# Rows scaled in place and turned by TensorE transposes, and the first key products set between the fourth and the fifth turned tile

## The chip, the cores and the metric

The kernel runs on one core of a Trainium2 chip. The metric is the device time of one execution in microseconds (us), from its start to its end. A profiled execution also has a span, from the first to the last instruction that the profiler recorded; the device time is a little longer than the span. Five engines work side by side, each through its own instructions in their order: PE (TensorE, matrix products; PEld is its weight loads), DVE (VectorE), ACT (ScalarE), POOL (GpSimd) and SP (SyncE, which issues the transfers). An engine whose next instruction waits runs nothing behind it.

## The reference

One layer of a small transformer: 1024 tokens of width 1024, 256 context tokens, everything in float32. The change touches the beginning, which is this part:

```python
def rmsnorm(x, g):
    y = xf * lax.rsqrt(jnp.mean(xf * xf, axis=-1, keepdims=True) + EPS)
    return y * g
def adaln(cond, w, b):
    return jax.nn.silu(cond) @ w + b
def modulate(h, shift, scale):
    return h * (1.0 + scale) + shift
...
hc = modulate(rmsnorm(ctx, g_pre_mix), csh1, csc1)      # context
pc = hc @ w_in[:, :COL_Q]
hx = modulate(rmsnorm(x, g_pre_mix), sh1, sc1)          # tokens
p = hx @ w_in                                           # keys, values, gates, queries, ...
```

So each row of `x` is multiplied by one over its root mean square, and each column (feature) then gets a scale and a shift that come from the condition vector `c` by a product with `w_ada`. Behind this follow a gated linear attention, a short convolution, an output projection and a convolutional feed-forward part, which the change leaves alone.

## The kernel before, in words

Tokens lie in eight tiles of 128 rows (`xs[0]` to `xs[7]`, 128x1024). The products need the features on the partitions, so each tile is turned: eight blocks of 128x128, one for each group of 128 features (`ft` 0 to 7). The turned and normed rows are collected in `xT[0]` (tiles 0 to 3, the half `hf` 0 of 512 tokens) and `xT[1]` (tiles 4 to 7, `hf` 1).

- `rms_diag(xt, eng)` (L250) sums the squares of a tile's rows on ACT (`act(..., AF.Square)`) or on DVE (L257), makes the reciprocal root on POOL (`rstd`, L200 and L201, two instructions), and multiplies the identity by it on POOL (L260). The result `dg` is a 128x128 diagonal.
- `turn(t)` (L328) multiplies each of the eight blocks by that diagonal on PE (L335), which turns and scales in one product; DVE copies one half of the result from the accumulation banks to `xT` (L341), ACT the other half.
- `ada_dot(j, ...)` (L226) makes one block of 128 shift or scale entries by a multiply-and-sum on DVE (L230), from a 512 KB block of `w_ada` loaded for it. Blocks `ft` and `8 + ft` belong to the features `ft`.
- `ada_affine(ft)` (L246) turns these into the final shift and scale in `am`, by two small ACT instructions.
- `norm_ft(ft, hf)` (L343) applies `am` on ACT to one feature group of 512 tokens (tile `t`), rounds it on ACT to the high part `hxh`, and leaves the low part `hxl` (L351, DVE) to be called later as `lo()`. Products in this kernel are made of three float32r products of high and low parts.
- `k_q(ft, hf)` (L353) makes the nine products of one unit: six from `hxh` and three that need `hxl` (L359 and L362), for the keys and the first queries. There are 16 units; `prep(n)` (L390) prepares a unit two ahead of the one that runs: `norm_ft`, one `ada_dot` for the next features, after the second of each pair `ada_affine`, and `lo()`.
- Behind these units come further query products (from L145 at 66.84 us in the trace), the value products, and among them the context tiles: `ctx_load` (L499) makes the diagonals of two context tiles, `ctx_norm` (L504) turns them by products with them (L514).

In this first part ACT, DVE, POOL and PE run their instructions in the order in which the code writes them (`tc.manual_schedule`); on SP the order of the transfers is the scheduler's. The tiles `x` take eight buffers; `xT[1]` and the later blocks of `w_ada` reuse them as they come free.

Of the kernel before, what the change touches and what calls it, by code (L numbers as in the profile page):

```python
# [8 lines left out]
F32 = mybir.dt.float32  # L9
# [11 lines left out]
CT = 256  # L21
# [98 lines left out]
def build(nc, ap, out, dbg=None):  # L120
# [3 lines left out]
    def nm(s="t"):  # L124
        return f"{s}{next(names)}"

    def act(o, i, fn=AF.Copy, **kw):
        return S.activation(o, i, fn, **kw)  # L128
# [20 lines left out]
    with tile.TileContext(nc) as tc, tc.manual_schedule(engines={mybir.EngineType.PE}):  # L149
# [25 lines left out]
        def bank(n):  # L175
            return pools[n][1].tile([P, 512], F32, tag=n, name=nm("ps"))
# [7 lines left out]
        def col(name, j=0, n=1):  # L184
            o, w = COLS[name]
            return cols[:, o + j : o + j + n]
# [57 lines left out]
        bsg = cp.tile([P, KT], F32, name="bsg")  # L244

        def ada_affine(ft):  # L246
            act(am[:, 0, ft, 0:1], gcol[:, ft : ft + 1], AF.Identity, bias=col("bada", ft))
            act(am[:, 1, ft, 0:1], gcol[:, 8 + ft : 9 + ft], AF.Identity, scale=col("g1", ft), bias=bsg[:, ft : ft + 1])

        def rms_diag(xt, eng=None):  # L250

            ss = cp.tile([P, 1], F32, tag="ss", bufs=4, name=nm("ss"))
            junk = pst.tile([P, D], BF16, tag="junk", bufs=1, name=nm("junk"))
            if eng is None:
                act(junk, xt, AF.Square, accum_out=ss)
            else:
                eng.tensor_tensor_reduce(junk, xt, xt, 1.0, 0.0, ALU.mult, ALU.add, ss)  # L257
            r = rstd(ss, 1, 1.0 / D)
            dg = pst.tile([P, P], F32, tag="dg", bufs=4, name=nm("dg"))
            G.tensor_scalar(dg, ident, r[:, 0:1], None, ALU.mult)  # L260
            return dg

        def x_load(src, t):
            xt = px.tile([P, D], F32, tag="x", name=nm("x"))
            SY.dma_start(xt, src[t * P : (t + 1) * P, :])
            return xt
# [61 lines left out]
        def turn(t):  # L328

            hf, ts_ = t // 4, slice(t % 4 * P, t % 4 * P + P)  # L330
            for g in range(2):
                pt = bank((ps_mm, ps_at)[g])
                for j in range(4):
                    ft = 4 * g + j
                    PE.matmul(pt[:, j * P : (j + 1) * P], xs[t][:, ft * P : (ft + 1) * P], dgs[t], start=True, stop=True)  # L335
                for q in range(2):
                    o, i = xT[hf][2 * g + q][:, :, ts_], pt[:, 256 * q : 256 * q + 256].rearrange("p (f t) -> p f t", f=2)
                    if g:
                        act(o, i)
                    else:  # L340
                        V.tensor_copy(o, i)  # L341
# [23 lines left out]
        with tc.manual_schedule(engines={mybir.EngineType.Activation, mybir.EngineType.DVE, mybir.EngineType.Pool}):  # L365
# [11 lines left out]
                V.tensor_copy(cbs[0][:, n * 512 : n * 512 + 512], pb)  # L377
# [32 lines left out]
            V.tensor_scalar(bsc1, col("bada", 8, 8), 1.0, None, ALU.add)  # L410
            V.tensor_tensor(bsg, bsc1, col("g1", 0, 8), ALU.mult)
# [12 lines left out]
            xT[1] = [px.tile([P, 2, 512], F32, tag="x", name=nm("xT")) for _ in range(4)]  # L424
            turn(4)
            for raw, pg in zip((wk0, wq0_), pgs):
                act(pg[0][:, :2], raw[:, :2])
            turn(5)
            for raw, pg in zip((wk0, wq0_), pgs):
                V.tensor_tensor(pg[1][:, :2], raw[:, :2], pg[0][:, :2].bitcast(F32), ALU.subtract)  # L430
            ada_dot(1, 0, adas[1][0])
            lo = norm_ft(0, 0)
            turn(6)
            lo()
            turn(7)
# [33 lines left out]


        aT = pgt.tile([NG, T + CT], F32R, name="aT")
        V.memset(aT[96:NG, :].bitcast(F32), 1.0)
        wgr = pst.tile([NG, 2 * QK], F32, tag="t", bufs=4, name="wgr")
        SY.dma_start(wgr, ap["wg"])
        wgh, wgl = (pgt.tile([NG, 2 * QK], F32R, name=n) for n in ("wgh", "wgl"))
# [18 lines left out]
            act(e, e, AF.Ln, bias=one)  # L494
            V.scalar_tensor_tensor(g, pg, 0.0, e, ALU.min, ALU.subtract)

        cxs, cdg, hch, hcl = [], [], [], []

        def ctx_load():  # L499
            for j in range(NCT):  # L500
                cxs.append(x_load(ap["ctx"], j))
                cdg.append(rms_diag(cxs[j]))

        def ctx_norm(f2):  # L504

            if f2 % 2 == 0:
                hch.append(px.tile([P, 4, CT], F32R, tag="x", name=nm("hch")))
                hcl.append(px.tile([P, 4, CT], F32R, tag="x", name=nm("hcl")))
            tt = pst.tile([P, 2, CT], F32, tag="t", bufs=4, name=nm("t"))
            pt = bank(ps_at)  # L510
            for f1 in range(2):
                ft = 2 * f2 + f1
                for j in range(NCT):
                    PE.matmul(pt[:, f1 * CT + j * P : f1 * CT + (j + 1) * P],  # L514
                              cxs[j][:, ft * P : (ft + 1) * P], cdg[j], start=True, stop=True)
# [1155 lines left out]
```

## Time and profile before

| what | value |
|---|---|
| runs | 1153.4, 1157.13 and 1157.71 us, median 1157.13 |
| profiled execution, device time | 1157.1 us |
| its span | 1155.3 us |
| TensorE clock granted, mean | 0.993 |
| PE busy | 97% of the span |
| DVE, ACT, POOL busy | 76%, 46%, 43% |
| first product with `dg` | 7.72 us |
| first key product | 26.84 us |
| first product behind the 16 units | 66.84 us |

In lines of the timeline the first number is the start in us from the beginning of the span, the second the time from there to the end of the row's last instruction, then engine, line, operation, what it writes and reads, the shapes, and the number of instructions; in square brackets stands how long the engine was idle before and what ended that. A product of two float32 tiles shows as two matrix instructions, a transpose as one.

### The profile page before, as it was taken

Reading aid. Unit: us, or ns where it says so; the run is one execution under the profiler, and the core shown is the slowest. Engines: PE = TensorE matmul, PEld = TensorE weight load, DVE = VectorE, ACT = ScalarE, POOL = GpSimd, SP = SyncE. Lnnn points to the kernel's source line nnn. Section 1 sums busy time; section 2 is a strip of 40 time slices with the busy share of each in tenths; the row PEclk is TensorE's granted clock in tenths of the full one; section 3 lists DMA queues with packets and bytes.
Section 4 is the critical chain, followed back from the end, with each engine's and each line's share of the span. In section 5 each row is a group of like instructions: output and inputs, shape, how many; then the busy total and the mean of one; then the engine's idle time right before and its main releaser. Section 6 shows DMA issues by size and latency. Waiting matters only on the chain. (4 is left out here: it accounts for less than half of the span.)

```text
span 1155.3 us, 16916 instructions
## 1 busy us (share of the span) xinstructions
PE 1120.4 (97%) x6272; PEld 927.1 (80%) x6272; DVE 872.3 (76%) x1182; ACT 528.9 (46%) x957; POOL 498.9 (43%) x467
## 2 busy tenths in 40 slices
PE   8899988999999999999999999999999999999997
PEld 6689977888887878887878788888887888888885
DVE  5876657899778556576888978787878787777676
ACT  6845156644344456655233242433333345544443
POOL 5211012347466111128777868687767780000002
PEclk9999999999999999999999999999999999999999
DMA  9884853522113283232343323232323169978572
GB/s 345 311 277 137 275 143 119 149 63 60 46 44 102 59 280 113 79 110 73 91 146 110 109 92 119 92 110 92 119 91 110 66 208 338 357 250 273 195 245 100
DMA packets 80132, 176.00 MB, mean 152 GB/s; under 512 B 9807, under 2 KB 21711, under 8 KB 80050
## 3 DMA queue, kind: packets, MB, share of 16 engines
q1 hardware_dynamic: 80050, 174.93, 45.9%
q8 instruction: 49, 0.80, 0.3%
q14 instruction: 33, 0.27, 0.1%
HBM read 142.12 MB, written 32.78 MB: 151 GB/s over the span
## 5 line engine op out<-in xcount | busy, mean ns | idle before, releaser
L1343 DVE SCALAR_TENSOR_TENSOR y<-u,cols,y 128x945 f32<-128x945 f32 (+2 forms) x176 | 214.8, 1222 | 3.7 <-ACT y L128 1.3
L145 PE MATMUL ps<-mx,p 128*128 128x512 f32 x440 | 174.3, 396 | 4.1 <-DVE g L1398 2.2
L146 PE MATMUL ps<-mx,p 128*128 128x512 f32 x440 | 173.1, 394 | 0.0
L147 PE MATMUL ps<-mx,p 128*128 128x512 f32 x440 | 173.1, 393 | 0.0
L135 POOL TENSOR_TENSOR p<-rs,p 128x512 fp32r<-128x512 f32 x88 | 115.3, 1314 | 88.3 <-ACT p L128 84.5
L643 POOL TENSOR_TENSOR wl<-wr,wh 128x256 fp32r<-128x256 f32 x64 | 62.0, 998 | 158.9 <-ACT wh L128 158.7
L147 PE MATMUL ps<-p,p 128*128 128x512 f32 x308 | 120.1, 390 | 0.2
L146 PE MATMUL ps<-p,p 128*128 128x512 f32 x308 | 120.0, 390 | 0.0
L145 PE MATMUL ps<-p,p 128*128 128x512 f32 x308 | 119.9, 389 | 0.0
L145 PE MATMUL ps<-hxh,wh 128*128 128x512 f32 x256 | 104.5, 408 | 1.2 <-DVE sc L701 1.2
L145 PEld LDWEIGHTS ps<-mx,p 128*128 128x128 f32 x440 | 83.1, 189 | 27.0 <-ACT u L128 5.7
L230 DVE CUSTOM_DVE_ANT_0 ada<-ada,cb 128x1024 f32<-128x1024 f32 x64 | 80.3, 1265 | 31.3 <-DMA ada<-in_ada 30.7
L146 PE MATMUL ps<-hxl,wh 128*128 128x512 f32 x256 | 100.6, 393 | 0.0
L147 PE MATMUL ps<-hxh,wl 128*128 128x512 f32 x256 | 100.5, 393 | 0.0
L128 ACT ACTIVATE p<-rs 128x512 fp32r<-128x512 f32 x88 | 54.5, 623 | 100.5 <-POOL rs L1193 100.5
L147 PEld LDWEIGHTS ps<-mx,p 128*128 128x128 f32 x440 | 83.1, 189 | 18.6
L146 PEld LDWEIGHTS ps<-mx,p 128*128 128x128 f32 x440 | 83.0, 189 | 18.1
L135 POOL TENSOR_TENSOR p<-wr,p 128x512 fp32r<-128x512 f32 x58 | 76.1, 1312 | 13.0 <-ACT p L128 13.0
L128 ACT ACTIVATE y<-u,cols 128x1024 f32<-128x1024 f32 x22 | 26.6, 1210 | 107.1 <-DVE u L1405 107.1
L145 PE MATMUL ps<-b,p 128*128 128x512 f32 x176 | 69.5, 395 | 0.0
L146 PE MATMUL ps<-b,p 128*128 128x512 f32 x176 | 69.4, 394 | 0.0
L147 PE MATMUL ps<-b,p 128*128 128x512 f32 x176 | 69.4, 394 | 0.0
(277 smaller groups left out, 2598.9 us busy)
## 6 DMA issues: line engine op xcount, KB each, us to landing
ada<-in_ada SPq DMA_DIRECT2D x64, 512.0 KB, 4.6
wr<-in_wu SPq DMA_DIRECT2D x48, 512.0 KB, 4.0
h<-hd SPq DMA_DIRECT2D x77, 256.0 KB, 4.5
hd<-h SPq DMA_DIRECT2D x73, 256.0 KB, 2.2
wdr<-in_wd SPq DMA_DIRECT2D x55, 256.0 KB, 3.7
wdr<-in_wd SPq DMA_DIRECT2D x22, 512.0 KB, 5.9
x<-in_x SPq DMA_DIRECT2D x16, 512.0 KB, 4.4
wr<-in_wb SPq DMA_DIRECT2D x16, 512.0 KB, 3.7
```

Of the source, the lines that this page charges most:

```text
L128: return S.activation(o, i, fn, **kw)
L135: (eng or V).tensor_tensor(lo, raw, hi.bitcast(F32), ALU.subtract)
L145: PE.matmul(ps, lh, rh, start=first, stop=False, skip_group_check=more)
L146: PE.matmul(ps, lh, rl, start=False, stop=False, skip_group_check=more)
L147: PE.matmul(ps, ll, rh, start=False, stop=last, skip_group_check=more)
L230: V.tensor_tensor_reduce(raw, raw, cbs[which], 1.0, 0.0, ALU.mult, ALU.add, dst)
L643: eng.tensor_tensor(lo[:, k : k + 2], raw[:, k : k + 2], hi[:, k : k + 2].bitcast(F32), ALU.subtract)
L1343: V.scalar_tensor_tensor(y3[:, ro, co], u3[:, ri, ci], col("wcf", 9 * p + 3 * (dr_ + 1) + dc + 1), y3[:, ro, co], ALU.mult, ALU.add)
```

## The change

- `rms_diag` becomes `rms_rows`: no diagonal is made; the tile's rows are multiplied by the reciprocal root in place, on DVE or (argument `seng=S`) on ACT. The turns on PE are transposes against the identity, one instruction each. The two context tiles are treated in the same way.
- Sums of squares of tiles 5 and 7 go to DVE with the scaling on ACT; tiles 0 to 3, 4 and 6 have the sum on ACT and the scaling on DVE.
- The code interleaves the first four tiles one at a time with their turns. `norm_ft(0, 0)` and the first unit `k_q(0, 0)` come ahead of most of tiles 4 to 7: `rms_rows` of 4 and 5 and `turn(4)` stand ahead of `k_q(0, 0)`, the rest behind it. In `turn` both halves of tiles 4 to 7 use the two banks of `ps_at`, as the four of `ps_mm` are the key banks by then.
- The two instructions of `ada_affine` go from ACT to POOL (and `bsg` is not needed any more).
- Transfers: the first two blocks of `w_ada` and the first weights are issued ahead of `x` tiles 4 to 7.
- The memset of two rows of `aT` goes from DVE to POOL.

```diff
-        def ada_affine(ft):
-            act(am[:, 0, ft, 0:1], gcol[:, ft : ft + 1], AF.Identity, bias=col("bada", ft))
-            act(am[:, 1, ft, 0:1], gcol[:, 8 + ft : 9 + ft], AF.Identity, scale=col("g1", ft), bias=bsg[:, ft : ft + 1])
+            G.tensor_scalar(am[:, 0, ft, 0:1], gcol[:, ft : ft + 1], col("bada", ft), None, ALU.add)
+            G.tensor_scalar(am[:, 1, ft, 0:1], gcol[:, 8 + ft : 9 + ft], bsc1[:, ft : ft + 1], col("g1", ft), ALU.add, ALU.mult)
...
-        def rms_diag(xt, eng=None):
+        def rms_rows(xt, eng=None, seng=V):
...
             r = rstd(ss, 1, 1.0 / D)
-            dg = pst.tile([P, P], F32, tag="dg", bufs=4, name=nm("dg"))
-            G.tensor_scalar(dg, ident, r[:, 0:1], None, ALU.mult)
-            return dg
+            if seng is V:
+                V.tensor_scalar(xt, xt, r[:, 0:1], None, ALU.mult)
+            else:
+                act(xt, xt, scale=r[:, 0:1])
...
-                pt = bank((ps_mm, ps_at)[g])
+                pt = bank(ps_at if t > 3 or g else ps_mm)
...
-                    PE.matmul(pt[:, j * P : (j + 1) * P], xs[t][:, ft * P : (ft + 1) * P], dgs[t], start=True, stop=True)
+                    PE.transpose(pt[:, j * P : (j + 1) * P], xs[t][:, ft * P : (ft + 1) * P], ident)
...
-            xs += [x_load(ap["x"], t) for t in range(4, 6)]
             adas = {0: [ada_load(j, pa, "a", 16) for j in (0, 8)]}
-            xs += [x_load(ap["x"], t) for t in range(6, NT)]
             wk0, wq0_ = wk_load(0, 2), wq_load(0, 0, pkq, "qh", 2)
+            xs += [x_load(ap["x"], t) for t in range(4, NT)]
...
-            dgs = [rms_diag(xs[t]) for t in range(4)]
+            rms_rows(xs[0])
             V.tensor_scalar(bsc1, col("bada", 8, 8), 1.0, None, ALU.add)
+            rms_rows(xs[1])
             turn(0)
-            dgs.append(rms_diag(xs[4], V))
+            rms_rows(xs[2])
             turn(1)
-            dgs.append(rms_diag(xs[5]))
+            rms_rows(xs[3])
             turn(2)
             ada_dot(0, 0, adas[0][0])
             turn(3)
             ada_dot(8, 0, adas[0][1])
             ada_affine(0)
-            dgs.append(rms_diag(xs[6], V))
-            dgs.append(rms_diag(xs[7]))
             pgs = wk_pages(0), wq_pages(wq0)
-            turn(4)
...
+            rms_rows(xs[4])
+            rms_rows(xs[5], V, S)
+            turn(4)
             k_q(0, 0)
+            rms_rows(xs[6])
+            turn(5)
+            rms_rows(xs[7], V, S)
+            turn(6)
+            ada_dot(1, 0, adas[1][0])
+            turn(7)
...
-                cdg.append(rms_diag(cxs[j]))
+                rms_rows(cxs[j])
...
-                    PE.matmul(pt[:, f1 * CT + j * P : f1 * CT + (j + 1) * P],
-                              cxs[j][:, ft * P : (ft + 1) * P], cdg[j], start=True, stop=True)
+                    PE.transpose(pt[:, f1 * CT + j * P : f1 * CT + (j + 1) * P], cxs[j][:, ft * P : (ft + 1) * P], ident)
```

First ACT, between the rounding of the first unit (`hxh` of features 0, tokens 0 to 511) and that of the second (`hxh` in the last row). Before; `xT<-ps` are the copies of turned tiles, `t` and `hxh` the two steps of `norm_ft`, and the numbers behind the names are those of single buffers:

```order
L128 ACTIVATE t_325<-xT_152,am 128x512
L128 ACTIVATE hxh_323<-t_325 128x512
L128 ACTIVATE xT_288<-ps_335 128x2x128
L128 ACTIVATE xT_289<-ps_335 128x2x128
L128 ACTIVATE xT_288<-ps_350 128x2x128
L128 ACTIVATE xT_289<-ps_350 128x2x128
L128 ACTIVATE t_380<-xT_286,am 128x512
L128 ACTIVATE hxh_323<-t_380 128x512
```

And ACT in the same place now, from the rounding of the first unit on (`junk,ss` is a sum of squares; the four copies of tiles 6 and 7 and the second unit follow behind the last row):

```order
L128 ACTIVATE hxh_250<-t_252 128x512
L128 ACTIVATE junk_269,ss_268<-x_136 128x1024
L128 ACTIVATE x_138<-x_138,rstd_278 128x1024
L128 ACTIVATE xT_260<-ps_289 128x2x128
L128 ACTIVATE xT_261<-ps_289 128x2x128
L128 ACTIVATE junk_306,ss_305<-x_140 128x1024
L128 ACTIVATE xT_260<-ps_319 128x2x128
L128 ACTIVATE xT_261<-ps_319 128x2x128
L128 ACTIVATE x_142<-x_142,rstd_329 128x1024
```

Two sums of squares (tiles 4 and 6) and two scalings (tiles 5 and 7) have moved behind the rounding of the first unit, with the copies of the turned tiles between them.

Then DVE from the low part of the first unit (`hxl`) on, now; `ISA junk,ss` is the sum of squares of tiles 5 and 7, `COPY xT` the copies of turned tiles, `TENSOR_SCALAR x` the scaling of tiles 4 and 6:

```order
L350 TENSOR_TENSOR hxl_251<-t_252,hxh_250 128x512
L258 TENSOR_SCALAR x_136<-x_136,rstd_271 128x1024
L255 ISA junk_276,ss_275<-x_138 128x1024
L255 ISA ss_275 128x1
L340 COPY xT_258<-ps_282 128x2x128
L340 COPY xT_259<-ps_282 128x2x128
L258 TENSOR_SCALAR x_140<-x_140,rstd_308 128x1024
L340 COPY xT_258<-ps_312 128x2x128
L340 COPY xT_259<-ps_312 128x2x128
L255 ISA junk_327,ss_326<-x_142 128x1024
L255 ISA ss_326 128x1
```

Before, DVE had behind the low part of the first unit only the copies of the last tile and the next `ada_dot`:

```order
L351 TENSOR_TENSOR hxl_324<-t_325,hxh_323 128x512
L341 COPY xT_286<-ps_343 128x2x128
L341 COPY xT_287<-ps_343 128x2x128
L230 ISA ada_147,gcol<-ada_147,cb_107 128x1024
L230 ISA gcol 128x1
```

The sums and scalings of tiles 4 to 7 thus alternate between ACT and DVE, each in the engine's one queue. The third place is PE at the first unit: `turn(4)` (a row for each half of a tile) stands ahead of it, and `turn(5)` begins right behind its nine products, ahead of the second unit:

```order
L334 MATMUL ps_282<-ident,x_136 128x128 x4
L334 MATMUL ps_289<-ident,x_136 128x128 x4
L358 MATMUL ps_262<-hxh_250,wah_244 128x512
L358 MATMUL ps_264<-hxh_250,wah_244 128x512
L358 MATMUL ps_266<-hxh_250,wqh_246 128x512
L361 MATMUL ps_262<-hxh_250,wal_245 128x512
L361 MATMUL ps_264<-hxh_250,wal_245 128x512
L361 MATMUL ps_266<-hxh_250,wql_247 128x512
L361 MATMUL ps_262<-hxl_251,wah_244 128x512
L361 MATMUL ps_264<-hxl_251,wah_244 128x512
L361 MATMUL ps_266<-hxl_251,wqh_246 128x512
L334 MATMUL ps_312<-ident,x_138 128x128 x4
```

Tiles 6 and 7 follow behind the last row, and then the second unit. Before, all eight turns stood ahead of the first unit.

More of the change, by code (lines that the diff above doesn't have):

```diff
@@ L242, in ada_affine_ctx @@
             V.tensor_tensor(am[:, 1, ft : ft + 4, 1], am[:, 1, ft : ft + 4, 1], col("g1", ft, 4), ALU.mult)
-        bsg = cp.tile([P, KT], F32, name="bsg")
         def ada_affine(ft):
-            act(am[:, 0, ft, 0:1], gcol[:, ft : ft + 1], AF.Identity, bias=col("bada", ft))
-            act(am[:, 1, ft, 0:1], gcol[:, 8 + ft : 9 + ft], AF.Identity, scale=col("g1", ft), bias=bsg[:, ft : ft + 1])
-        def rms_diag(xt, eng=None):
+            G.tensor_scalar(am[:, 0, ft, 0:1], gcol[:, ft : ft + 1], col("bada", ft), None, ALU.add)
+            G.tensor_scalar(am[:, 1, ft, 0:1], gcol[:, 8 + ft : 9 + ft], bsc1[:, ft : ft + 1], col("g1", ft), ALU.add, ALU.mult)
+        def rms_rows(xt, eng=None, seng=V):
             ss = cp.tile([P, 1], F32, tag="ss", bufs=4, name=nm("ss"))
@@ L420, in build @@
             ada_affine(0)
-            dgs.append(rms_diag(xs[6], V))
-            dgs.append(rms_diag(xs[7]))
             pgs = wk_pages(0), wq_pages(wq0)
-            xT[1] = [px.tile([P, 2, 512], F32, tag="x", name=nm("xT")) for _ in range(4)]
-            turn(4)
             for raw, pg in zip((wk0, wq0_), pgs):
                 act(pg[0][:, :2], raw[:, :2])
-            turn(5)
+            lo = norm_ft(0, 0)
             for raw, pg in zip((wk0, wq0_), pgs):
                 V.tensor_tensor(pg[1][:, :2], raw[:, :2], pg[0][:, :2].bitcast(F32), ALU.subtract)
-            ada_dot(1, 0, adas[1][0])
-            lo = norm_ft(0, 0)
-            turn(6)
             lo()
-            turn(7)
+            xT[1] = [px.tile([P, 2, 512], F32, tag="x", name=nm("xT")) for _ in range(4)]
             pk = [bank(ps_mm) for _ in range(4)]
             pq = [bank(ps_ms) for _ in range(2)]
+            rms_rows(xs[4])
+            rms_rows(xs[5], V, S)
+            turn(4)
             k_q(0, 0)
+            rms_rows(xs[6])
[4 more added lines that the diff above has]
+            turn(7)
             load_ada(2)
@@ L471, in build @@
         aT = pgt.tile([NG, T + CT], F32R, name="aT")
-        V.memset(aT[96:NG, :].bitcast(F32), 1.0)
+        G.memset(aT[96:NG, :].bitcast(F32), 1.0)
         wgr = pst.tile([NG, 2 * QK], F32, tag="t", bufs=4, name="wgr")
@@ L495, in logdecay @@
             V.scalar_tensor_tensor(g, pg, 0.0, e, ALU.min, ALU.subtract)
-        cxs, cdg, hch, hcl = [], [], [], []
+        cxs, hch, hcl = [], [], []
         def ctx_load():
```

1 line of the change is left out of this document (removed).

## The prediction

> **What bounds the kernel now.** I read the page first, then the busy time of the engines by stretches, then who waited for whom on PE, then the timeline of the beginning.
>
> ```profile
> PE 1120.4 (97%) x6272; PEld 927.1 (80%) x6272; DVE 872.3 (76%) x1182; ACT 528.9 (46%) x957; POOL 498.9 (43%) x467
> ```
>
> ```profile
> 26.80:66.80 40.00, 36.10 (x147) 26.31 (x146) 30.73 (x47) 31.82 (x58) 10.18 (x9) 1.00 0.90 311
> 66.80:84.00 17.20, 17.20 (x99) 15.29 (x99) 13.50 (x27) 7.50 (x19) 0.00 (x0) 1.00 0.81 277
> 84.00:125.00 41.00, 41.00 (x336) 40.86 (x335) 27.24 (x61) 18.10 (x53) 5.61 (x8) 1.00 0.51 172
> ```
>
> The columns behind the stretch and its length are the busy time of PE, PEld, DVE, ACT and POOL, then the clock, the DMA share and GB/s. From 66.8 us PE never stops for 58 us, so a microsecond by which the first product at 66.84 moves is a microsecond of the end, and one of PE's work less between 84 and 125 us is too. Ahead of that PE is not the bound. These are its products around the units (`k_q`):
>
> ```profile
> 25.04 2.05 PE L335 MATMUL ps<-dg,x 128*128 128x128 f32 x16 [0.74 <-POOL dg L260]
> 26.84 0.70 PE L359 MATMUL ps<-hxh,wah 128*128 128x512 f32 x2
> ...
> 29.20 0.73 PE L359 MATMUL ps<-hxh,wah 128*128 128x512 f32 x2
> ...
> 64.80 0.62 PE L359 MATMUL ps<-hxh,wah 128*128 128x512 f32 x2
> ...
> 66.84 0.39 PE L145 MATMUL ps<-hxh,wqh 128*128 128x512 f32 x1
> ```
>
> A unit takes PE 2.04 us (64.80 to 66.84), the 15 units behind the first would take 30.6, and they take 66.84 - 29.20 = 37.6. For 7.0 us they wait:
>
> ```profile
> PE ps L359 <- ACT hxh L128: 2.7, 6, 0.9
> PE ps L362 <- DVE hxl L351: 1.0, 2, 0.5
> ```
>
> The recorded waits are only part of it, as PE's ends are modelled, but they name what is late: the rounding on ACT and the low part on DVE. So the beginning is decided by how soon ACT and DVE have the rows of the second half of the tokens, and PE's turns matter only where they stand in that chain.
>
> **The first four tiles.** The prices, from ACT, DVE and POOL in the timeline and from the groups by line:
>
> ```profile
> 4.88 1.06 ACT L128 ACTIVATE junk<-x 128x1024 bf16<-128x1024 f32 x1 [1.68 <-DMA x<-in_x]
> 5.84 0.18 ACT L128 ACTIVATION_READ_ACCUMULATOR junk<-x 128x1 f32 x1
> ...
> 14.28 0.66 ACT L128 ACTIVATE xT<-ps 128x256 f32<-128x256 f32 x2 [2.07 <-PE ps L335]
> ...
> 23.09 0.81 ACT L128 ACTIVATE t<-xT,am 128x512 f32<-128x512 f32 x1
> 23.94 0.63 ACT L128 ACTIVATE hxh<-t 128x512 fp32r<-128x512 f32 x1
> ...
> 28.52 0.63 ACT L128 ACTIVATE hxh<-t 128x512 fp32r<-128x512 f32 x1
> ```
>
> ```profile
> 9.97 0.17 DVE L410 TENSOR_SCALAR bsc<-cols 128x8 f32<-128x8 f32 x1 [2.21 <-DMA cols<-in_cols]
> ...
> 11.31 1.23 DVE L257 CUSTOM_DVE_ANT_0 junk<-x 128x1024 bf16<-128x1024 f32 x1 [0.30 <-POOL dg L260]
> ...
> 16.98 0.75 DVE L341 COPY xT<-ps 128x256 f32<-128x256 f32 x2
> 17.65 1.22 DVE L230 CUSTOM_DVE_ANT_0 ada<-ada,cb 128x1024 f32<-128x1024 f32 x1
> ```
>
> ```profile
> 6.12 0.19 POOL L200 TENSOR_SCALAR rstd<-ss 128x1 f32<-128x1 f32 x1 [5.70 <-DVE cb L377]
> 6.40 0.55 POOL L201 TENSOR_TENSOR rstd<-rstd,small 128x1 f32<-128x1 f32 x1
> 7.04 0.63 POOL L260 TENSOR_SCALAR dg<-ident,rstd 128x128 f32<-128x128 f32 x1
> ```
>
> ```profile
> L128 ACT ACTIVATE y<-u,cols 128x1024 f32<-128x1024 f32 x22 | 26.6, 1210 | 107.1 <-DVE u L1405 107.1
> L1105 DVE TENSOR_SCALAR xn<-x,rstd 128x1024 f32<-128x1024 f32 x7 | 5.3, 754 | 9.7 <-POOL rstd L201 8.1 <-ACT xn L128 1.5
> ```
>
> A sum of squares is 1.15 us on ACT (4.88 to 6.02) and 1.22 on DVE; the root costs 0.95 from the sum's end at 6.02 to the start of what uses it (7.04, less the step between); two copies 0.66 on ACT and 0.75 on DVE; a dot 1.22. The scaling on DVE is the same operation and shape as L1105, 0.75. On ACT no row has it: 1.06 (one pass over the same tile, with a sum) to 1.21 (one with scale and bias); I take 1.06. The diagonal's 0.63 goes, but the 0.75 that replaces it moves to DVE or ACT.
>
> PE's turns, as products and as transposes, each with the product that follows:
>
> ```profile
> 89.98 1.05 PE L514 MATMUL ps<-dg,x 128*128 128x128 f32 x8
> 90.80 0.37 PE L145 MATMUL ps<-wah,hxh 128*128 128x272 f32 x1
> ```
>
> ```profile
> 430.39 1.03 PE L1124 MATMUL ps<-ident,xn 128*128 128x128 f32 x8
> 431.18 0.48 PE L145 MATMUL ps<-woh,mh 128*128 128x512 f32 x1
> ```
>
> Four products with the diagonal hold PE 0.82 us in eight passes, eight transposes 0.79: a transpose is one pass of 0.10 us. But PE has two paces. Passes of L335 by stretch:
>
> ```profile
> 7.70:10.27 2.57, 2.55 (x12) 2.55 (x13) 1.00 1.02 400
> ...
> 13.40:15.45 2.05, 2.05 (x21) 2.05 (x20) 1.00 1.03 412
> ```
>
> After idling, 0.21 us a pass (2.57 us for 12); after some 5 us of steady work little over half of it, though the clock column says 1.00. The new turns come in short pieces, so I price them at 0.21 on the way to the first unit: 1.7 us for a tile, 2.0 with the last one's landing. The Trainium skill (TensorE: Matmul & The Clock Gate, Part 4: PE-mode transpose) says that transposes do not count as work for that gate. No row here shows transposes alone; by its rule the turns stay at the slow pace, as in my sum; were they fast, 1.5 us would come off in the two turns on the path.
>
> Now `bsc1` stands ahead of the scaling of tile 1 on DVE, so that waits for `cols` until 10.1. ACT sums tile 3 behind the copies of `turn(1)`: scaling 0.75, turn 2.0, copies 0.66, sum 1.15, root 0.95, together 5.5, and tile 3's scaling starts at 15.6 and ends at 16.35. DVE then copies tile 2 (0.7), does a dot (1.15), copies tile 3 (0.7) and does the second dot (1.22): 20.1. POOL makes `am`: 0.3, and up to 0.6 behind a subtraction on DVE, say 20.9; ACT's two steps (0.85 and 0.63) end at 22.4. Before, that was 24.57. So the first unit's input is 2.2 us earlier.
>
> **The second half.** From there every step waits for the one before, as each engine's queue alternates. Sum of tile 4 on ACT 1.15, root 0.95, scaling on DVE 0.75, sum of tile 5 on DVE behind it 1.22, root 0.95, scaling on ACT 1.06, copies of `turn(4)` behind it 0.66, sum of tile 6 1.15, root 0.95, scaling on DVE 0.75, copies of `turn(5)` behind it 0.75, sum of tile 7 1.22, root 0.95, scaling on ACT 1.06: 13.6. Then the copies of `turn(6)` free the second bank (0.66), four transposes fill it (0.85), copies 0.66, and the two steps of `norm_ft(0, 1)` 1.45: 17.2 in all. The second unit starts at 22.4 + 17.2 = 39.6 instead of 29.20: **+10.4**. `k_q(0, 0)` and the turns on PE fit into this with room, so the earlier first unit gains nothing. All that is queued behind on DVE, the dots of the next features first, waits too.
>
> **The other 15 units.** `ada_affine` leaves ACT, which takes off at most the 2.7 us for which PE waited for the rounding. Two scalings of context tiles come onto DVE, 1.5. And PE meets the second unit after a gap of three to four us. Such a gap, and the clock behind it:
>
> ```profile
> 156.84 0.79 PE L486 MATMUL ps<-wgh,aT 98*128 98x512 f32 x1 [2.35 <-DVE gc L495]
> ```
>
> ```profile
> 156.80:158.50 1.70, 1.67 (x4) 1.38 (x5) 1.70 (x3) 0.84 (x2) 0.00 (x0) 0.50 0.00 0
> ```
>
> A half clock for some 3.3 us costs 1.6. These three cancel nearly; I keep 37.6 for the 15 units, **0**. The lower bound is PE's own pace, 30.6 and 1.6, that is -5.4; the upper bound comes with the third rival.
>
> **The context tiles.** Sixteen products become transposes: 4 x (0.82 - 0.39) = **-1.7**, in full, since PE is busy for 41.00 of 41.00 us there. The memset of `aT` leaves an idle DVE for an idle POOL: nothing. The transfers are issued in another order, but tile 4 still comes before 16 us (1.4 MB more ahead of a tile that DVE reads at 11.31 before, at the 400 GB/s of the row above, are 3.5 us), and its sum starts at 22: hidden.
>
> The sum: 1157.1 + 10.4 + 0 - 1.7 = **1165.8 us**. The profiled execution (1157.1) stands at the runs' median (1157.13), so nothing is to be corrected. 0.5% is 5.8 us, about what a measurement of this kernel can tell from no change.
>
> **The rivals.**
> 1. Faster: the steps of tiles 4 to 7 overlap, and only ACT's own work lies between the two units. That is 2 x 1.15 + 2 x 1.06 + 4 x 0.66 + 1.45 = 8.5, the second unit at 30.9, and with the 15 units at PE's pace of 30.6 the first product behind them at 61.5: 1157.1 - 5.3 - 1.7 = 1150.1. It decides if the chain is shorter than 6.8 us (29.20 - 22.4). For it speak the 97% of PE on the page, and half the passes for its turns. Against it: each root needs its sum, each scaling its root, and the queues have them in turn. Chance 0.04.
> 2. No change that can be told: the chain is as computed, but the units behind it run without waits, as ACT and POOL have been relieved and transfers have had 10 us to come: -5.4, 1160.4. For it: DVE is busy for 30.73 of 40 us, so it isn't full. Against it: the waits in the units come from DVE's dots, low parts and splits, which stay. Chance 0.20.
> 3. Slower still: `am` on POOL waits for DVE. Rows:
>
> ```profile
> 11.37 1.22 POOL L200 TENSOR_SCALAR rstd<-ss 128x1 f32<-128x1 f32 x1
> ...
> 17.86 2.55 POOL L260 TENSOR_SCALAR dg<-ident,rstd 128x128 f32<-128x128 f32 x1
> ```
>
> The first is a 0.19 us operation that ends just after the DVE sum of 11.31, the second a 0.63 us one beside two of DVE's. If each second `am` waits through a low part and a dot in place of a low part alone, each pair of units is 1.22 later: seven times, +8.5, 1174.3. The Trainium skill (SBUF — State Buffer, Who interferes with whom) calls the port that DVE and GpSimd share an exclusive lock, and names DVE operations with two inputs in SBUF; the first row agrees. Whether POOL gets in between two DVE operations decides. Chance 0.14.
>
> That the change does not do what it says I exclude: the transposes of L1124 are eight records for a tile's eight blocks.
>
> **How the numbers follow.** The forecast has 0.62. Slower by over 0.5% (above 1162.9) are the forecast and the third rival, 0.76; within 0.5% the second, 0.20; faster the first, 0.04. The range leaves out the first rival and the outer half of the third: 1159.5, a little below the second, to 1172.5, where `am` costs most of the third's price.
>
> **What would show it.** Right: the second unit near 39.6 us, ACT waiting for POOL between tiles 4 and 7 and PE idle for some 8 us around 30 to 39; the first product behind the units near 77; the context's transposes at half the products' time. The first four tiles are wrong if the first `hxh` is not within a microsecond of 22.4; the chain is wrong if tiles 5 and 7 are scaled while 4 and 6 are summed; the forecast falls if the second unit starts ahead of 33 us, or the units behind it take under 33 us.

## The result, and the profile after

The changed kernel takes 1172.22 us (median of five runs, 1170.77 to 1174.14) against 1157.13 (five runs, 1153.4 to 1158.16): the ratio is 1.0129, with a 95% interval of 1.0114 to 1.0144. The profiled execution has 1170.77 us and a span of 1168.9, 13.6 more than before. In the timeline of PE these rows answer to those around the units; the first two are the turns of tiles 2 and 3:

```profile
13.91 1.09 PE L334 MATMUL ps<-ident,x 128*128 128x128 f32 x8 [1.40 <-DVE x L258]
16.00 1.97 PE L334 MATMUL ps<-ident,x 128*128 128x128 f32 x8 [1.00 <-DVE x L258]
25.05 1.94 PE L334 MATMUL ps<-ident,x 128*128 128x128 f32 x8 [7.08 <-DVE x L258]
26.64 1.20 PE L358 MATMUL ps<-hxh,wah 128*128 128x512 f32 x2
...
29.93 1.04 PE L334 MATMUL ps<-ident,x 128*128 128x128 f32 x8
32.24 1.06 PE L334 MATMUL ps<-ident,x 128*128 128x128 f32 x8 [1.28 <-DVE xT L340]
35.38 1.66 PE L334 MATMUL ps<-ident,x 128*128 128x128 f32 x8 [2.08 <-ACT x L128]
39.15 1.22 PE L358 MATMUL ps<-hxh,wah 128*128 128x512 f32 x2 [2.11 <-ACT hxh L128]
...
82.09 0.39 PE L145 MATMUL ps<-hxh,wqh 128*128 128x512 f32 x1
```

The first unit begins where it did (26.64 against 26.84), although its `hxh` is ready at 22.14, as `turn(4)` stands ahead of it on PE. Then three turns come one at a time, the second waiting for a bank and the third for a scaling, and the second unit begins at 39.15, not at 29.20: 9.95 us. Behind these waits stand the four scalings of tiles 4 to 7, on DVE and ACT in turn, each of which waited for its root from POOL:

```profile
24.15 0.75 DVE L258 TENSOR_SCALAR x<-x,rstd 128x1024 f32<-128x1024 f32 x1 [1.28 <-POOL rstd L201]
...
30.68 0.75 DVE L258 TENSOR_SCALAR x<-x,rstd 128x1024 f32<-128x1024 f32 x1 [3.75 <-POOL rstd L201]
```

```profile
27.00 1.15 ACT L128 ACTIVATE x<-x,rstd 128x1024 f32<-128x1024 f32 x1 [3.82 <-POOL rstd L201]
...
34.18 1.15 ACT L128 ACTIVATE x<-x,rstd 128x1024 f32<-128x1024 f32 x1 [2.52 <-POOL rstd L201]
```

The first product behind the units comes at 82.09, not at 66.84. Of these 15.25 us the second unit brings 9.95, so the other 15 units bring 5.3: they take 42.94 us, not 37.64. The row of the engines' stretches for exactly these units:

```profile
39.15:82.09 42.94, 36.38 (x136) 27.21 (x136) 31.04 (x48) 26.86 (x42) 21.06 (x19) 0.92 0.72 237
```

POOL, the last busy time ahead of the clock (0.92), has 21.06 us in 19 instructions where the row of 26.80 to 66.80 before had 10.18 in 9. Who waits for it is in the list of waits, for ACT and for PE (who waited, for whom, then us in total, how often, and the longest), and in the timelines of POOL, DVE and ACT:

```profile
ACT t L128 <- POOL am L246: 15.4, 7, 3.6
```

```profile
PE ps L334 <- DVE x L258: 11.4, 5, 7.1
PE ps L358 <- ACT hxh L128: 7.3, 5, 2.1
```

```profile
38.08 0.34 POOL L246 TENSOR_SCALAR am<-gcol,bsc,cols 128x1 f32<-128x1 f32 x1 [2.64 <-DVE gcol L230]
...
42.64 1.78 POOL L245 TENSOR_SCALAR am<-gcol,cols 128x1 f32<-128x1 f32 x1
44.47 1.77 POOL L246 TENSOR_SCALAR am<-gcol,bsc,cols 128x1 f32<-128x1 f32 x1
46.21 0.28 POOL L245 TENSOR_SCALAR am<-gcol,cols 128x1 f32<-128x1 f32 x1
49.72 1.77 POOL L246 TENSOR_SCALAR am<-gcol,bsc,cols 128x1 f32<-128x1 f32 x1 [3.23 <-DVE gcol L230]
```

```profile
43.14 1.21 DVE L230 CUSTOM_DVE_ANT_0 ada<-ada,cb 128x1024 f32<-128x1024 f32 x1
...
44.28 0.68 DVE L350 TENSOR_TENSOR hxl<-t,hxh 128x512 fp32r<-128x512 f32 x1
44.89 1.21 DVE L230 CUSTOM_DVE_ANT_0 ada<-ada,cb 128x1024 f32<-128x1024 f32 x1
46.03 0.08 DVE L230 DVE_READ_ACCUMULATOR2_ANT gcol<- 128x1 f32 x1
```

```profile
46.27 0.82 ACT L128 ACTIVATE t<-xT,am 128x512 f32<-128x512 f32 x1 [3.61 <-POOL am L246]
```

At 38.08, with DVE waiting, the second `am` takes 0.34 us. At 44.47 the same instruction takes 1.77 and ends at 46.24, just behind the dot of 44.89, whose sum is read out at 46.03: by its length it waited through the low part and through the dot behind it. Only then does `t` on ACT start, and with it the next `hxh` that PE waits for. ACT stood 15.4 us for `am`; before, with `am` on ACT itself, it stood 4.9 there for the dot. PE stood 7.3 for `hxh` (2.7 before), 2.1 of them ahead of the second unit.

The context part went as written down. Four transposes and what follows, in the timeline:

```profile
105.29 0.60 PE L514 MATMUL ps<-ident,x 128*128 128x128 f32 x4
105.64 0.37 PE L145 MATMUL ps<-wah,hxh 128*128 128x272 f32 x1
```

They hold PE for 0.35 us where the products held it for 0.82. From the first product behind the units to the first one with a context page (`hch`) it is 37.5 us, not 39.2. What lies behind the units is not equally long in every profiled execution (1086.8 us of the span in the changed kernel, 1082.8 in the one with a cleared column below, which is the same there), so the parts of the beginning are compared by their rows, and whole kernels by the ratios of their runs.

### The profile page after: what moved, and what is told of

Same layout as the page of the kernel before. It is cut to its first block, busy times and chain, and to the rows that moved or that the text cites. A ratio compares the mean times of both kernels' runs of the same rounds, so it can differ in the third digit from the quotient of the medians.

```text
span 1168.9 us, 16743 instructions
## 1 busy us (share of the span) xinstructions
PE 1117.2 (96%) x6192; PEld 921.0 (79%) x6192; DVE 874.5 (75%) x1188; ACT 526.1 (45%) x943; POOL 501.1 (43%) x474
```

## The experiments

Four questions were asked in turn: whether `am` alone is the 5.3 us, whether sums and roots are what holds the second unit, what order and way of scaling each cost by themselves, and what is left on the path. In each, "second unit" is its first product in the timeline of PE, and "units" the time from there to the first product behind them. "The changed kernel" has 39.15, 42.94 and a ratio of 1.0129.

**`am` back on ACT, the rest as changed.**

```diff
-            G.tensor_scalar(am[:, 0, ft, 0:1], gcol[:, ft : ft + 1], col("bada", ft), None, ALU.add)
-            G.tensor_scalar(am[:, 1, ft, 0:1], gcol[:, 8 + ft : 9 + ft], bsc1[:, ft : ft + 1], col("g1", ft), ALU.add, ALU.mult)
+            act(am[:, 0, ft, 0:1], gcol[:, ft : ft + 1], AF.Identity, bias=col("bada", ft))
+            act(am[:, 1, ft, 0:1], gcol[:, 8 + ft : 9 + ft], AF.Identity, scale=col("g1", ft), bias=bsg[:, ft : ft + 1])
...
```

> The changed kernel with one part undone: ada_affine is on ACT again (bsg is back), all else as changed. Theory A: the 5.3 us by which the 15 units behind the first grew (37.64 to 42.94 us) are the second am, which on POOL waits 1.8 to 2.8 us beside a low part and a dot of DVE, seven times, so that t on ACT waits 1.5 to 3.6 us each. Then the 15 units take 37 to 39 us, the second unit stays near 39.2 us, and the time is about 1167 us, 5 us under the changed kernel. Theory B: the units grew because the second unit now meets PE after idling (units of 3.8 us instead of 2.0 at half pace) and because the dots of DVE come later; then the 15 units stay at 42 to 43 us and the time at 1171 to 1173 us.

Measured: ratio 1.0069 (1.0057 to 1.0081), median 1163.95 us; second unit 40.29, units 37.53. The timeline of ACT:

```profile
45.51 0.39 ACT L128 ACTIVATE am<-gcol,bsg,cols 128x1 f32<-128x1 f32 x1 [1.05 <-DVE gcol L230]
45.93 0.82 ACT L128 ACTIVATE t<-xT,am 128x512 f32<-128x512 f32 x1
```

The dot ended at 45.48, `am` stands done at 45.9 and `t` follows at once. The units are 5.4 us shorter, and theory A holds: the other things that theory B named are all still there. But the second unit did not stay at 39.2: it comes 1.1 us later, as ACT now waits for the dot with `am` and rounds the first weights only behind it, so that the first `hxh` ends at 23.01, not at 22.14. So the first product behind the units moves by 4.3 us, from 82.09 to 77.82; the time fell by more than that, and the rest lies behind the units.

**`am` on POOL in the kernel before**, the reverse of that diff there, and nothing else.

> The kernel before with one part of the change alone: ada_affine is on POOL; diagonals, products and order as before. Theory A: am on POOL is late by itself, whatever the order ahead of it: second unit still near 29.2 us, the 15 units 42 to 43 us instead of 37.6, time about 1162 us, 5 us over before. Theory B: am on POOL is late only in the new order: 15 units within 1 us of 37.6, time 1156 to 1158 us.

Measured: ratio 1.0045 (1.0033 to 1.0057), median 1161.95; second unit 28.70, units 42.40. In the timelines of POOL and of ACT:

```profile
34.03 1.77 POOL L246 TENSOR_SCALAR am<-gcol,bsc,cols 128x1 f32<-128x1 f32 x1
```

```profile
35.84 0.81 ACT L128 ACTIVATE t<-xT,am 128x512 f32<-128x512 f32 x1 [3.62 <-POOL am L246]
```

It is the same 1.77, and units that are 4.8 us longer than before, without any of the new order. The first product behind the units comes at 71.10, 4.3 later than before, as the second unit is 0.5 earlier. So `am` on POOL costs some 5 us in the units and 4.3 us at their end, shown from both sides.

**One column cleared on DVE between the low part and the next dot**, in the changed kernel.

```diff
                 lo()
+                if hf:
+                    V.memset(gap, 0.0)
...
```

> The changed kernel with one added instruction per pair of units: DVE clears one column (128x1) between the low part that follows the second dot and the next dot, 0.1 us each. In the changed kernel the second am on POOL ends only with the next dot, 1.77 to 2.82 us. Theory A (POOL gets in as soon as DVE runs an instruction with no two inputs in SBUF): am ends behind the low part, 0.8 us or less in 5 of the 7 pairs, t starts a microsecond earlier, the 15 units take 39 us or less, time 1167 to 1169 us. Theory B (POOL gets in only where DVE stands still, whatever it runs): am still 1.7 us or more, 15 units 42 to 43 us, time 1171 to 1174 us.

Measured: ratio 1.0108 (1.0094 to 1.0123), median 1169.37, which can't be told from the changed kernel's; second unit 39.28, units 42.97. In the timelines of DVE and POOL:

```profile
44.59 1.78 POOL L247 TENSOR_SCALAR am<-gcol,bsc,cols 128x1 f32<-128x1 f32 x1
...
45.02 1.22 DVE L231 CUSTOM_DVE_ANT_0 ada<-ada,cb 128x1024 f32<-128x1024 f32 x1
45.04 0.06 DVE L401 MEMSET gap<- 128x1 f32 x1
```

`am` takes as long as ever, as theory B had it. The clearing shows as 0.06 us on top of the dot's start, so it opened no gap. Theory B's reason, that POOL gets in only where DVE stands still, says more than the rows do. In the changed kernel the first instruction of `am` (L245, at 42.64) waits through a low part and a dot too, but ends at 44.42, when DVE has gone on without a stop from the dot (43.14 to 44.35) to the next low part (44.28). What the six long `am` rows there share is that each ends 0.05 to 0.14 us behind the end of a dot, and none behind a low part. What lets them in there was not tested.

**Sums and roots of tiles 4 to 7 moved ahead**, the scalings left in their places.

```diff
             ada_dot(0, 0, adas[0][0])
+            rs = {4: rms_sum(xs[4])}
             turn(3)
             ada_dot(8, 0, adas[0][1])
+            rs[6] = rms_sum(xs[6])
             ada_affine(0)
...
+            for t in (5, 7):
+                rs[t] = rms_sum(xs[t], V)
             lo()
...
```

> The changed kernel with the sums of squares and the roots of tiles 4 to 7 moved ahead: those of tiles 4 and 6 on ACT stand ahead of the first unit's two steps, those of 5 and 7 on DVE behind the low parts of the first weights; the scalings, turns and units stay in their order, and a second buffer for the squares is added. Theory A (the chain sum, root, scaling, turn of the tiles in turn sets the second unit): of the 17.0 us between the first hxh and the second unit the four sums and roots go, 2 x 1.15 + 2 x 1.22 + 4 x 0.95 = 8.5, and some 2 us come back as the first hxh waits for two sums on ACT, and some 2 more as the turns then stand behind each other on PE and its two banks: second unit at 33 to 36 us instead of 39.15, time 4 to 6 us under the changed kernel, about 1167. Theory B (PE's turns in two banks set it): second unit within 1 us of 39.2, time 1171 to 1173.

Measured: ratio 1.0118 (1.0101 to 1.0135), median 1169.88; second unit 39.34, units 42.90. The theory's number failed. The timelines of POOL and of PE say why:

```profile
21.86 2.33 POOL L246 TENSOR_SCALAR am<-gcol,bsc,cols 128x1 f32<-128x1 f32 x1
```

```profile
28.82 1.20 PE L363 MATMUL ps<-hxh,wah 128*128 128x512 f32 x2
...
32.81 1.29 PE L339 MATMUL ps<-ident,x 128*128 128x128 f32 x8
34.60 1.06 PE L339 MATMUL ps<-ident,x 128*128 128x128 f32 x8 [0.50 <-DVE xT L345]
36.17 1.06 PE L339 MATMUL ps<-ident,x 128*128 128x128 f32 x8 [0.50 <-DVE xT L345]
```

The two sums on DVE held up the first `am` on POOL (2.33 us), so the first `hxh` ended at 25.7 instead of 22.14. And the turns of tiles 5 to 7 stand on PE behind the first unit, which takes 4.0 us, and are 1.6 to 1.8 apart. What the sums gave was lost again ahead of them and behind them.

**Both edits together.**

> Both edits together, on the changed kernel: sums and roots of tiles 4 to 7 moved ahead, and ada_affine on ACT. If the late second unit and the late am are two separate costs, they add: second unit at 33 to 36 us, the 15 units 37 to 39 us, time about 1162 us, 9 to 11 us under the changed kernel. If the units only take up slack that the early second unit leaves (one limit behind both, DVE's dots), the first product behind the units moves less than the sum of the two, to 78 us at best, and the time is 1166 or more.

Measured: ratio 1.0042 (1.0029 to 1.0054), median 1160.74; second unit 37.20, units 37.33. The first product behind the units comes at 74.53, 7.6 us earlier than in the changed kernel, so the units do not merely take up slack. It is more than the two edits gave one at a time (4.3 and nothing), since with `am` on ACT the early sums no longer hold up the first `am`. But with the first `hxh` at 23.3 the second unit still comes at 37.2, behind the 33 to 36 expected. By the rows PE is the next limit: it works through `turn(4)`, the first unit and three turns from 26.41 to 35.1 with no stop longer than 0.5 us. These 8 us that the second unit is still late are read from the rows; no run in this order took them out.

**The old order with scaled rows**: sums and roots where they stood before, each tile scaled right ahead of its turn.

```diff
-            dgs = [rms_diag(xs[t]) for t in range(4)]
+            rs = [rms_sum(xs[t]) for t in range(4)]
...
+            scale_rows(xs[0], rs[0])
             turn(0)
-            dgs.append(rms_diag(xs[4], V))
+            rs.append(rms_sum(xs[4], V))
+            scale_rows(xs[1], rs[1])
             turn(1)
...
```

> The order of the kernel before, with the scaled rows and the transposes of the change: sums and roots of all eight tiles where they stood before, each tile scaled right ahead of its turn (tiles 0 to 3, 5 and 7 on DVE, 4 and 6 on ACT), the context tiles as in the change, ada_affine on ACT. Theory A (what costs the second unit is the new place of tiles 4 to 7 in the program; scaling and transposing rows are cheap by themselves): three scalings more on the way of ACT and DVE to the first unit, 2 us, and the context's transposes -1.7; second unit at 30 to 33 us, time 1155 to 1160 us. Theory B (the scaled rows themselves cost, as each turn now waits for a scaling on DVE or ACT and PE meets the units after idling): second unit at 36 us or later, time 1162 us or more.

Measured: ratio 1.0098 (1.0085 to 1.0111), median 1168.03; second unit 43.66, units 36.59. Theory A fell: in the old order the rows cost more than in the new one. The timeline of DVE and of PE around tile 3:

```profile
18.70 0.76 DVE L357 COPY xT<-ps 128x256 f32<-128x256 f32 x2 [1.21 <-PE ps L351]
19.37 1.22 DVE L230 CUSTOM_DVE_ANT_0 ada<-ada,cb 128x1024 f32<-128x1024 f32 x1
...
20.51 0.75 DVE L262 TENSOR_SCALAR x<-x,rstd 128x1024 f32<-128x1024 f32 x1
...
22.47 0.76 DVE L357 COPY xT<-ps 128x256 f32<-128x256 f32 x2 [1.21 <-PE ps L351]
```

```profile
17.55 1.97 PE L351 MATMUL ps<-ident,x 128*128 128x128 f32 x8 [0.66 <-DVE x L262]
...
21.32 1.97 PE L351 MATMUL ps<-ident,x 128*128 128x128 f32 x8 [1.80 <-DVE x L262]
```

DVE scales a tile, stands for 1.21 us until PE has turned it, copies, and only then scales the next; PE stands meanwhile, 13.9 us in all between its eight turns, and each turn takes 1.97 us, 0.21 to 0.25 a transpose. No engine works ahead.

**The new order with diagonals and products**, `am` on ACT, to take the order alone.

```diff
-            rms_rows(xs[4])
-            rms_rows(xs[5], V, S)
+            dgs.append(rms_diag(xs[4]))
+            dgs.append(rms_diag(xs[5], V))
             turn(4)
             k_q(0, 0)
...
```

> The order of the change with the diagonals and products of before: tiles 0 to 7 are turned by products with a diagonal that POOL makes, tiles 4 to 7 behind the first unit, ada_affine on ACT, the context tiles as in the change. Four cases stand then beside each other for the second unit's start, order by way of scaling: 29.20 (old order, diagonals), 43.66 (old order, scaled rows), 40.29 (new order, scaled rows, am on ACT), and this one. Theory A (the new place of tiles 4 to 7 is what costs): 36 to 41 us, as the sums of tiles 6 and 7 still stand behind the copies of the turn before and the first unit stands between the turns. Theory B (scaling in place is what costs, by the queues of DVE and ACT): 29 to 33 us, and a time of 1153 to 1157 us.

Measured: ratio 1.0095 (1.0075 to 1.0116), median 1166.62; second unit 42.08, units 37.38. That is 1.1 us above theory A's 36 to 41 and far from theory B's 29 to 33: the order costs without any scaling in place. The timeline of ACT:

```profile
30.35 0.66 ACT L128 ACTIVATE xT<-ps 128x256 f32<-128x256 f32 x2 [6.11 <-PE ps L351]
30.90 1.06 ACT L128 ACTIVATE junk<-x 128x1024 bf16<-128x1024 f32 x1
```

The sum of tile 6 could have been made during the 6.11 us for which ACT stood, but it is written behind the copies of tile 4. Since the previous experiment showed that rows in the old order cost as much, neither the order nor the rows alone is the cause. What both have is that a step waits in a queue behind a step of the tile ahead.

**The same rows in the old order, each scaled one tile earlier.** If that is the cause, this should do away with it.

```diff
             scale_rows(xs[0], rs[0])
+            scale_rows(xs[1], rs[1])
             turn(0)
             rs.append(rms_sum(xs[4], V))
-            scale_rows(xs[1], rs[1])
+            scale_rows(xs[2], rs[2])
             turn(1)
...
```

> The kernel of the old order with scaled rows, in which the second unit began at 43.66 us, with each tile's scaling moved ahead of the turn before its own. Theory A (there DVE stands for 1.21 us in every turn, since scaling, transposes and copies of one tile wait for each other on its queue): with the scaling one tile ahead the transposes of a tile run beside the copies of the one before, 1.2 us less for each of six or seven turns, second unit at 35 to 37.5 us, time 1160 to 1163 us. Theory B (the sums and roots set it): second unit at 42 us or later, 1167 us.

Measured: ratio 0.9984 (0.9975 to 0.9994), median 1154.31; second unit 31.48, units 37.00. It is better than theory A had it, and under the kernel before. The timeline of PE and of DVE:

```profile
11.29 6.72 PE L351 MATMUL ps<-ident,x 128*128 128x128 f32 x32 [4.13 <-DVE x L262]
18.82 1.09 PE L351 MATMUL ps<-ident,x 128*128 128x128 f32 x8 [0.80 <-ACT x L128]
```

```profile
15.59 0.74 DVE L262 TENSOR_SCALAR x<-x,rstd 128x1024 f32<-128x1024 f32 x1
16.25 0.75 DVE L357 COPY xT<-ps 128x256 f32<-128x256 f32 x2
16.91 1.22 DVE L230 CUSTOM_DVE_ANT_0 ada<-ada,cb 128x1024 f32<-128x1024 f32 x1
```

PE turns four tiles without a stop and stands 4.5 us between its turns, not 13.9; DVE goes from scaling to copies to dot without waiting. The same instructions in another order are 1.1% apart, some 13 us. Against the kernel before nothing is gained in the beginning itself: the first product behind the units comes at 68.48, 1.6 us later than there, and the transposes of the context make up for it.

**Rows scaled on POOL**, in the old order: `G.tensor_scalar(xt, xt, r[:, 0:1], None, ALU.mult)` in place of the diagonal, so that no step is added to DVE or ACT.

> The old order with scaled rows, the scaling on POOL, where the diagonals were made, so that the queues of DVE and ACT are those of before. What a 128x1024 scaling takes on POOL no run here has shown; the nearest row, a low part of 128x512 with two inputs, took 1.28 us alone and 1.9 beside DVE, so an estimate is 1.3 to 4 us each. At 1.3 the second unit would be near 30 and the time 1155 to 1157; at 4 us POOL alone needs 32 us and 6 for the roots, the second unit comes at 44 us or later, time 1168 or more.

Measured: ratio 1.0092 (1.0077 to 1.0107), median 1167.05; second unit 42.03. The timeline of POOL:

```profile
14.70 2.85 POOL L275 TENSOR_SCALAR x<-x,rstd 128x1024 f32<-128x1024 f32 x1
...
18.59 2.85 POOL L275 TENSOR_SCALAR x<-x,rstd 128x1024 f32<-128x1024 f32 x1
```

2.85 us a tile, between the estimate's ends, and 3.9 with the root: eight of them fill POOL until 37 us. The diagonals, an eighth as wide, took 0.61 to 0.63 us there.

**PE kept busy ahead of the second unit** by nine products whose results are not used, in the changed kernel with `am` on ACT.

```diff
             turn(6)
+            busy(5)
             ada_dot(1, 0, adas[1][0])
             turn(7)
+            busy(4)
...
```

> The changed kernel with ada_affine on ACT, and PE kept busy ahead of the second unit: five products of 128x512 more behind the turn of tile 6 and four behind that of tile 7, into a bank that the second unit starts anew, so that the output does not change. There the second unit took 4.0 us where later ones take 2.04. Theory A (that half pace is on the path): the second unit takes 2.1 to 2.5 us, everything behind it comes 1.5 to 2 us earlier, time about 1162. Theory B (ACT and DVE set the third unit whatever PE does): the second unit is shorter but the third starts within 0.7 us of 44.3, no difference in the time (1163.5 to 1164.5).

Measured: ratio 1.0087 (1.0072 to 1.0102), median 1166.54; second unit 39.41. The stretch of 38 to 42 us, without and with these products:

```profile
38.00:42.00 4.00, 1.89 (x5) 1.42 (x5) 2.99 (x5) 3.75 (x9) 0.69 (x1) 0.50 0.40 137
```

```profile
38.00:42.00 4.00, 2.60 (x11) 1.61 (x9) 2.53 (x5) 3.94 (x10) 1.57 (x1) 1.00 0.48 133
```

The granted clock is 1.00 instead of 0.50, and the third unit begins at 42.07 instead of 44.30. So far theory A. But the first product behind the units comes at 77.62, where it was 77.82: later units wait for ACT and DVE and give it all back, and the time is not shorter (the interval overlaps that without the nine products). By theory B's reason, though later than it said, the half clock is no part of the time lost, as far as the kernel with `am` on ACT shows it.

**The context tiles alone**, scaled and transposed in the kernel before.

```diff
-                cdg.append(rms_diag(cxs[j]))
+                scale_rows(cxs[j], rms_sum(cxs[j]))
...
```

> The kernel before with the context part of the change alone: the two context tiles are scaled on DVE and transposed, tiles 0 to 7 and ada_affine as before. By the prediction's term the sixteen transposes take 1.7 us off PE's work between the first product behind the units and the first with a context page (39.16 us before, 37.5 then); the two scalings on DVE may put 0 to 1.5 us onto the units. Theory A: the scalings are hidden, 1154 to 1155 us, 1.7 under before. Theory B: they are not, 1156 us, no difference.

Measured: ratio 0.9989 (0.9978 to 1.0000), median 1154.5. The stretch from the first product behind the units (66.72) to the first with `hch` (104.2) is 37.5 us, not 39.2; the units take 37.94 against 37.64, so the two scalings cost 0.3 at most. The gain is at the edge of what the runs can tell, and its size that of theory A.

**A version to beat both**: the kernel before, context tiles scaled on ACT and transposed, `am` on DVE.

```diff
-            act(am[:, 0, ft, 0:1], gcol[:, ft : ft + 1], AF.Identity, bias=col("bada", ft))
+            V.tensor_scalar(am[:, 0, ft, 0:1], gcol[:, ft : ft + 1], col("bada", ft), None, ALU.add)
...
```

> A version that may beat both: the kernel before, with the context tiles scaled on ACT and transposed, and ada_affine on DVE right behind the second dot instead of ACT. Theory A: transposes -1.7, and t on ACT no longer waits behind am there, another 0 to 1 us: 1153 to 1155 us. Theory B: am's two small instructions on DVE, 0.2 us each, delay the low parts and the next dots by as much as ACT gains: 1155 to 1157 us.

Measured: ratio 0.9979 (0.9970 to 0.9989), median 1154.25; second unit 28.19, units 37.39. This one is faster than the kernel before by 0.1 to 0.3%. Its interval and that of the rows one tile ahead overlap; the two were not joined.

## Why the prediction was right, and where it was not

The direction was right and the time inside the range, but near its upper end: 1172.22 is 6.4 us above the forecast, 0.3 below the end of the range, and nearer to the third rival's 1174.3 than to the forecast. The range was said to leave out the outer half of the third rival, which would have ended it at 1170.1; the end written down, 1172.5, leaves out only the outer 1.8 us. So the forecast was right for a little over half of the loss (8.7 of 15.1 us), and that the range holds the rest is owed to where its end was put. By the prediction's own steps:

- **The first four tiles**: the first `hxh` was to end at 22.4 us and ends at 22.14. Right, also in that the earlier input of the first unit gains nothing.
- **The second half**: the chain was to take 17.2 us and the second unit to start at 39.6, +10.4. It takes 17.0 (22.14 to 39.15), +9.95. It is also the chain that was described: by its terms the scalings of tiles 4 to 7 start 2.1, 5.0, 8.8 and 12.5 us behind the first `hxh`, and they start 2.0, 4.9, 8.5 and 12.0 behind it. The parts that differ are small: the scaling on ACT takes 1.15, not 1.06. PE stood some 5.5 us between 30 and 39, not 8. That such waits cost is shown by the one-tile-ahead version of the old order, in which they are taken out and the second unit goes from 43.66 to 31.48; for the changed kernel's own order, moving the sums gave 3.1 us (with `am` on ACT, 40.29 to 37.20), with the turns and the first unit on PE as the next limit. What that order would give with those moved too was not tried.
- **The context tiles**: -1.7 forecast, -1.65 measured, and -1.7 in the kernel that has only this.
- **The other 15 units**, put at **0**, is the step that failed: they cost +5.3. The three parts that were to cancel are each small: `am` off ACT was credited with up to 2.7 and is worth 0.6 in the units (37.39 and 37.94 with `am` on DVE and on ACT, where the place of the context scalings differs too), the two context scalings were charged 1.5 and cost 0.3, the half clock was charged 1.6, makes the second unit 1.8 longer (3.83 against 2.04) and is not on the path. What is there instead is the third rival, `am` on POOL waiting through a low part and a dot, to which 0.14 was given. It was priced at 1.22 for each of seven pairs, 8.5 in all; five of the seven waited like this or longer (1.77 to 2.82 us), and 5.3 came. Forecast and third rival with this measured size make 1157.1 + 10.4 + 5.3 - 1.7 = 1171.1; the profiled run had 1170.8. The row that decided it was among those quoted: 2.55 us for a 0.63 us instruction of POOL beside two of DVE. It was read as one possibility, and it held for most pairs.
- **The clock of PE.** The rule of the Trainium skill (TensorE: Matmul & The Clock Gate, Part 4: PE-mode transpose), that transposes do not engage the gate's full rate, does not hold for these float32 transposes: in the version one tile ahead 32 of them without a gap took 0.21 us each, and the next eight ran at 0.10 to 0.14 (1.09 us with the last one's landing), with nothing but transposes ahead of them for 7 us. When the faster pace comes is open. In the old order, with gaps of 0.66 us and more, all eight turns took 1.97. But in the changed kernel the turn at 13.91 took 1.09 behind a gap of 1.40 us, and the next, at 16.00, took 1.97 behind a gap of 1.00. So the gaps alone do not decide it. (In the prediction's rows of L335 the faster pass is 0.10 us against 0.21, a little under half, not over.)
- **The port of DVE and POOL.** The Trainium skill (SBUF — State Buffer, Who interferes with whom) has an exclusive lock that goes to whoever issues first. The lock agrees with the six long `am` rows. Whether the first to issue gets it the rows do not settle: at 44.47 the row of `am` begins before that of the dot at 44.89, and the dot went ahead, but no row shows when either was issued.

## What to carry to other kernels

A small instruction moved to POOL is not free because POOL is idle: beside two-input instructions of DVE back to back it took 1.77 to 2.82 us here, not 0.3, so an instruction that somebody waits for belongs behind its producer on the same engine. Where two engines share the steps of a tile, count how often a step is written behind one that waits for another engine: the same scalings and transposes cost 1.0% right ahead of their turns and, one tile earlier, came out 0.2% under the kernel before, no more than the context's transposes give. And when a view shows an instruction at four times its length, price the change with that row too and not only with the short one.

## What was not expected of the hardware

- POOL's instruction on a 128x1 column, 0.28 to 0.34 us alone, took 1.77 us beside two DVE instructions and 2.82 beside three; a one-column clearing on DVE between them, 0.06 us, did not let it in.
- A scaling of 128x1024 takes 2.85 us on POOL, against 0.75 on DVE and 1.15 on ACT.
- In the changed kernel with `am` on ACT, where PE had only turns with gaps between the first unit and the second, its granted clock was 0.50 between 38 and 42 us; with nine more products there it was 1.00, with no gain at the end of the units.
